# Splits and loads of an attention encoder in another order: key parts one per period, first casts of the drain, output weights ahead of the next chunk's rows

## The chip, the cores and the metric

The kernel runs on one core of one Trainium2 chip. The metric is the device time of one execution in microseconds. Engines are named as in the profile: PE (TensorE), DVE (VectorE), ACT (ScalarE), POOL (GpSimd) and SP (SyncE, which here only issues DMAs, in order).

## What is computed

A two-layer encoder runs over a prompt of 2048 tokens and a sample of 512 tokens, each of 1024 channels, in float32. Layer 0 is windowed attention with 16 heads, 4 key-value heads, blocks of 128 queries, a bias by relative position, a sink logit per head and a SiLU gate. Layer 1 mixes by a Fourier transform over positions and channel groups, gated as well. The core of layer 0, cut:

```python
h = rmsnorm(x, g)
z = h @ w_in                       # q, k, v and gate, one product
scores = einsum("bnqhgd,bnkhd->bnhgqk", q, k) * scale + bias   # |i-j| <= 128
p = exp(scores - m); p = p / (sum(p) + exp(sink - m))
o = einsum("bnhgqk,bnkhd->bnqhgd", p, v)
return x + (o * silu(gate)) @ w_out
```

## The kernel before

Every float32 product is made of three products of halves: an operand is split into a high half, which ACT makes by a cast to fp32r, and a low half, which DVE or POOL makes by subtracting the high half from the operand. `matmul3` (L137) multiplies the halves; `beside` (L522) takes two products at a time, one on the upper and one on the lower 64 rows of the array, and lets their matmuls alternate.

Layer 0 works through five chunks of 512 tokens: chunk 0 is the sample, chunks 1 to 4 are the prompt. A chunk begins with `make_h` (the rows xk of x transposed are loaded by SP at L275, multiplied by the inverse norm on POOL at L277, split by ACT at L281 and DVE at L282) and `kv_proj` (keys into kwin, values into v). Then a loop `for n in range(19)` runs: 16 periods and three of drain. Each period executes a list of names, `PERIOD` for chunks 1 to 4 and `FIRST` for chunk 0; beside each name stands how many periods back its unit lies. Calls of `seq` chain the instructions of each engine in the order of this list, so that the list is the order of the work. One unit is half of a head pair's work. The names:

- S1 and S2 are the score products (PE, L655, into the banks spt). b1a to b2b add the bias and find the maximum (DVE, L674, CUSTOM), e1a to e2b are the exponentials (ACT, L682), r1 and r2 the reciprocals (DVE, L688), m1a to m2b the divides (DVE, L697 and L701; ACT, L695).
- T0 and T1 transpose the probabilities into the one buffer tp (PE, L714); hi0, hi1 (ACT, L727) and lo0, lo1 (DVE, L731) split tp into pts. T1 can write tp only when lo0 has read it.
- AV1 and AV2 multiply by the values (PE, L755); they need lo1 and lo0. t2, add, mul, sp and lop take the result on to uT (ACT L775, DVE L785, POOL L791, ACT L796, POOL L800).
- A and B are the projections of later heads (PE, L522): q and gate go into two banks, pj0 and pj1, alternately. qH and qL evacuate them: in chunks 1 to 4 by `evac_q` (ACT L565 reads the bank for the high half, DVE L566 reads it again for the low half) or `evac_g`; for the head pair p = 1 by `evac_first`, where ACT copies the bank (L579), ACT casts the copy (L580) and DVE subtracts (L581). In chunk 0 the list's "sc" reads the bank first, DVE L585 for q and L596 for the gate s, and qH and qL follow on the copy (L590, L601).
- W and WL split weights (ACT L180, POOL L185); "side" does odd jobs in chunk 0, late weights (POOL L937) and the key parts.

Key parts: in chunk 0 the keys lie in two buffers kt; eight parts of them have to be split into kwin, high half by ACT (L401) and low half by DVE (L402), both in `part_k`. Two are done before the loop, six at "side" in the first four periods, two, two, one and one.

Between two chunks stands the output projection of the chunk before (`out_proj`): eight steps of products of uT with wo, whose second half of the weights (wo_1_0 to wo_1_6) is loaded by `rest`, its first step, into four buffers. SP issues loads in order, and each waits for its buffer. In chunks 2 to 4 `make_h` comes ahead of `rest` and the other steps.

Of the kernel before, what the change touches and what calls it, by code (L numbers as in the profile page):

```python
# [20 lines left out]
P = 128  # L21
# [34 lines left out]
def encoder(  # L56
# [150 lines left out]
    def attention_phase():  # L207

        with ExitStack() as es:
# [5 lines left out]
            def stats(c):  # L215

                tok, lo_t, hi_t = CHUNKS[c]
                nt = min(640, hi_t - tok) // P
                ss = main.tile([P, 8], F32, tag="ss", bufs=2, name=f"ss{c}")

                xs = []

                def one(i):

                    if i:
                        sq = ACT.activation(xs[i - 1], xs[i - 1], AF.Square, accum_out=ss[:, i - 1 : i])

                        if c > 1:
                            seq(ACT, sq)
                        else:  # L230
                            after(sq, last_exp[0])
                    while len(xs) < min(nt, i + (2 if c > 1 else 1)):
                        t = len(xs)
                        xs.append(xtile([P, D], F32, f"xs{c}_{t}"))
                        after(SP.dma_start(xs[t], x[tok + t * P : tok + (t + 1) * P, :]), last_exp[0] or last_x[0])

                return [lambda i=i: one(i) for i in range(nt + 1)] + [
                    lambda: inv_rms(ss, nt, f"inv{c}", lambda ins: seq(DVE, ins) if c > 1 else None)
                ]

            def spread_all(c, inv):
# [146 lines left out]
            def kv_proj(c, hs, halo, norms=None, early=None):  # L388
# [9 lines left out]
                def part_k(t, j, rows, src):  # L398
                    kw, sp = kwin[2 * t + j], src[j * 64 : j * 64 + 64, :n]
                    cs = slice(own0 + P, own0 + P + n)  # L400
                    hi = ACT.copy(kw[rows, 0, cs], sp)  # L401
                    lo = DVE.tensor_tensor(kw[rows, 1, cs], sp, f32(kw[rows, 0, cs]), ALU.subtract)  # L402
                    if PE in chain:
                        seq(ACT, hi)
                        seq(DVE, lo)

                def evac_k(t, ps, n, wc):
                    ps = scaled(ps, invb, f"k{t}")
# [66 lines left out]
                if norms is not None:  # L475
                    for t in range(2):
                        kt = main.tile([P, 512], F32, tag="xr", bufs=3, name=f"kt{c}_{t}")
                        DVE.tensor_tensor(kt, kps[t], invb[:, :CH], ALU.mult)
                        for j in range(2):
                            for rows in (slice(0, 64), slice(64, 128)):  # L480
                                k_splits.append(lambda t=t, j=j, rows=rows, kt=kt: part_k(t, j, rows, kt))
                    for _ in range(2):
                        k_splits.pop(0)()
                if halo:
                    pt = spt[0][:, :256]
                    for t in range(2):
# [49 lines left out]
            def qg_proj(c, which, p, bank, hs, res, invb=None):  # L536

                n = 12 + p if which == "g" else p
                st = {}

                def fetch():
                    if "w32" not in st:
                        st["w32"] = fetch_w(n, f"{which}{c}_{p}")

                def high():
                    st["w"], low = split_w(c, n, f"{which}{c}_{p}", st["w32"])
                    return low

                def load():
                    st["w"] = load_w(c, n, f"{which}{c}_{p}", None if p else DVE, w32=st.get("w32"))  # L550

                def left(k):
                    ks = slice(k * P, (k + 1) * P)
                    return [t[:, ks] for t in st["w"]]

                out = Product(bank, left, lambda k: hs[k])

                def pair_of():
                    qab = ap.tile([P, 2, CH], F32R, align_bytes=LINE, tag="qab", bufs=2, name=f"qab{c}_{p}")
                    res["q"] = qab  # L560
                    return qab

                def evac_q():
                    st["qab"] = qab = pair_of()
                    seq(ACT, ACT.activation(qab[:, 0], out.ps, AF.Copy, scale=-0.125))  # L565
                    return lambda: seq(DVE, DVE.scalar_tensor_tensor(  # L566
                        qab[:, 1], out.ps, -0.125, f32(qab[:, 0]), ALU.mult, ALU.subtract
                    ))

                def evac_g():  # L570
                    th = ap.tile([P, CH], F32, tag="tmp", bufs=2, name=f"th{c}_{p}")
                    seq(ACT, ACT.activation(th, out.ps, AF.Tanh, scale=0.5))
                    s = res["s"] = ap.tile([P, CH], F32, tag="s", bufs=2, name=f"s{c}_{p}")
                    return lambda: seq(DVE, DVE.scalar_tensor_tensor(s, th, 1.0, out.ps, ALU.add, ALU.mult))

                def evac_first():
                    whole = ap.tile([P, CH], F32, tag="tmp", bufs=2, name=f"q{c}_{p}")
                    qab = pair_of()
                    seq(ACT, ACT.activation(whole, out.ps, AF.Copy, scale=-0.125))  # L579
                    seq(ACT, ACT.copy(qab[:, 0], whole))  # L580
                    return lambda: seq(DVE, DVE.tensor_tensor(qab[:, 1], whole, f32(qab[:, 0]), ALU.subtract))  # L581

                def normed_q():
                    whole = ap.tile([P, CH], F32, tag="tmp", bufs=2, name=f"q{c}_{p}")
                    place(DVE.scalar_tensor_tensor(whole, out.ps, -0.125, invb[:, :CH], ALU.mult, ALU.mult))  # L585

                    def high():
                        qab = pair_of()
                        seq(ACT, ACT.copy(qab[:, 0], whole))
                        return lambda: seq(DVE, DVE.tensor_tensor(qab[:, 1], whole, f32(qab[:, 0]), ALU.subtract))  # L590

                    return high

                def normed_g():
                    s = res["s"] = ap.tile([P, CH], F32, tag="s", bufs=2, name=f"s{c}_{p}")
                    place(DVE.tensor_tensor(s, out.ps, invb[:, :CH], ALU.mult))  # L596

                    def high():
                        th = ap.tile([P, CH], F32, tag="tmp", bufs=2, name=f"th{c}_{p}")
                        seq(ACT, ACT.activation(th, s, AF.Tanh, scale=0.5))  # L600
                        return lambda: seq(DVE, DVE.scalar_tensor_tensor(s, th, 1.0, s, ALU.add, ALU.mult))  # L601

                    return high

                def place(ins):
                    if PE in chain:
                        seq(DVE, ins)

                if invb is None:
                    evac = evac_g if which == "g" else evac_first if p == 1 else evac_q  # L610
                else:
                    evac = normed_g if which == "g" else normed_q
                return fetch, high, load, out, evac
# [453 lines left out]
            for c in range(len(CHUNKS)):  # L1067

                if c > 1:
                    hs, halo = make_h(c, invb)  # L1070
                for s in tail:
                    s()
# [73 lines left out]
                def side(n):  # L1146
                    if n in (1, 3):
                        side_steps.append(late_w(n // 2))
                    elif n in (2, 4):
                        side_steps.pop()()  # L1150
                    for _ in range((2, 2, 1, 1)[n] if n < 4 else 0):
                        k_splits.pop(0)()

                side_steps = []
                low_q, high_q, low_w = [], [], []
                for n in range(19):
                    if c == 0:
# [6 lines left out]
                    chain.setdefault(PE, None)  # L1164
                    first, second = fills(n)
                    if n == 16:
                        beside(*first[:2])
                        first = first[2:]
                    for name, back in PERIOD if c else FIRST:
                        m = n - back  # L1170
                        if name == "A":
                            beside(*first)
# [13 lines left out]
                        elif name == "WL":  # L1186
                            if low_w:
                                low_w.pop()()
                        elif name == "side":
                            side(n)  # L1190
                        elif name == "qL":
                            if low_q:
                                low_q.pop()()
                        elif name[:5] == "extra":
                            if n < 17:
                                for i in range(4 * n + 2 * int(name[5]), 4 * n + 2 * int(name[5]) + 2):
                                    extra(i)
                        elif 0 <= m < 16 and (name, m) != ("AV2", 15):
                            at[m // 2].ops[2 * (m % 2)][name]()
# [1073 lines left out]
```

## Time and profile before

| | |
|---|---|
| median of 3 runs | 1572.89 us (1572.43 to 1573.58) |
| the profiled execution | 1573.11 us |
| its span | 1571.3 us |
| granted TensorE clock | 0.999 |
| busy: PE, DVE, ACT, POOL | 98%, 73%, 57%, 29% of the span |

The rows of the profile read as follows. A timeline row gives the start in us, the duration in us, the engine, the line of the kernel, the operation, the tiles (out<-in) with their shape and a count, and in brackets how long the engine sat idle ahead of it and what ended that. A row of the waits gives the engine and line that waited, what it waited for, the total in us, how often, and the longest. A row of the groups gives the total busy time in us and the mean of one instruction in ns, then the idle time ahead.

### The profile page before, as it was taken

How to read it: one execution, taken by the hardware profiler on the slowest of the kernel's cores; microseconds unless marked ns; L12 is line 12 of the kernel's file. 1: busy time of each engine (PE TensorE's matmuls, PEld its weight loads, DVE VectorE, ACT ScalarE, POOL GpSimd, SP SyncE). 2: the span in 40 equal slices, each digit the busy share in tenths (PEclk: the TensorE clock that was granted, in tenths of full speed). 3: DMA queues.
4: the chain of work that ended last, by engine and by line, in shares of the span. 5: the costliest groups of instructions: out<-in, count | busy, mean ns of one | idle time of the engine just before them, and what ended most of it. 6: DMA issues, size and time to landing. Idle time of an engine off the chain costs nothing.

```text
span 1571.3 us, 33415 instructions
## 1 busy us (share of the span) xinstructions
PE 1545.5 (98%) x12958; PEld 1352.9 (86%) x12958; DVE 1147.0 (73%) x2503; ACT 892.3 (57%) x1960; POOL 454.1 (29%) x616
## 2 busy tenths in 40 slices
PE   9899999999999999999999999999999999999998
PEld 7799888999898888988888899988888888888886
DVE  5788655777637777367764477758999888989886
ACT  6788634777327785257861477746566564333353
POOL 2566562421413313314214142223121211101100
PEclk9999999999999999999999999999999999999999
DMA  8577687774766765856738666665575669656852
GB/s 327 208 273 232 218 344 276 230 277 168 280 237 203 253 217 188 335 199 196 264 130 337 234 224 233 233 250 192 211 251 184 205 239 397 211 201 246 298 193 94
DMA packets 100730, 372.70 MB, mean 237 GB/s; under 512 B 11235, under 2 KB 22251, under 8 KB 83420
## 3 DMA queue, kind: packets, MB, share of 16 engines
q1 hardware_dynamic: 82716, 297.38, 54.6%
q0 software_dynamic: 16688, 70.04, 11.3%
q10 hardware_dynamic: 1168, 3.15, 0.6%
q8 instruction: 102, 1.67, 0.4%
q14 instruction: 56, 0.46, 0.1%
HBM read 280.06 MB, written 90.47 MB: 236 GB/s over the span
## 4 chain that ended last, share of the span: by engine, by line
PE 83%; DVE 6%; DMA 5%; ACT 2%; issue 2%; POOL 1%; SPq 0%; POOLq 0%; DVEq 0%; ACTq 0%
PE pj L522 25%; PE av L755 6%; PE W L137 6%; PE pj L137 5%; PE spt L655 5%; PE tp L137 5%; PE av L137 5%; PE tp L714 4%; PE Wo L137 3%; PE spt L137 3%; PE Z L137 3%; PE fo L137 2%; PE z L1386 2%; PE Zo L137 2%; PE X L137 1%
## 5 line engine op out<-in xcount | busy, mean ns | idle before, releaser
L522 PE MATMUL pj<-h,wg 64*128 64x512 f32 x1920 | 438.7, 389 | 1.9 <-DVE s L596 1.9
L522 PE MATMUL pj<-h,wq 64*128 64x512 f32 x1560 | 379.7, 389 | 3.2 <-DVE q L585 3.2
L522 PEld LDWEIGHTS pj<-h,wg 64*128 64x128 f32 x1920 | 330.9, 184 | 26.7 <-DVE s L596 2.6
L522 PEld LDWEIGHTS pj<-h,wq 64*128 64x128 f32 x1560 | 284.4, 184 | 21.9 <-DVE q L585 3.9
L674 DVE CUSTOM_DVE_ANT_0 S<-spt,b 128x385 f32<-128x385 f32 (+1 forms) x320 | 165.3, 525 | 94.3 <-PE spt L655 90.8
L682 ACT ACTIVATE S<-S 128x385 f32<-128x385 f32 (+1 forms) x320 | 189.3, 592 | 64.8 <-DVE S L674 42.7
L727 ACT CAST pts<-tp 128x768 fp32r<-128x768 f32 (+1 forms) x160 | 121.2, 757 | 94.9 <-PE av L755 59.6
L731 DVE TENSOR_TENSOR pts<-tp,pts 128x768 fp32r<-128x768 f32 (+1 forms) x160 | 144.0, 900 | 13.2 <-ACT pts L727 12.4
L755 PE MATMUL av<-pts,v 64*128 64x256 f32 x1680 | 141.8, 287 | 0.4 <-DVE pts L731 0.4
L755 PEld LDWEIGHTS av<-pts,v 64*128 64x128 f32 x1680 | 126.3, 186 | 4.1 <-DVE pts L731 0.6
L800 POOL TENSOR_TENSOR uT<-o,uT 128x256 fp32r<-128x256 f32 x75 | 55.7, 743 | 247.0 <-ACT uT L796 246.7
L655 PE MATMUL spt<-kwin,qab 64*128 64x384 f32 (+1 forms) x960 | 121.1, 338 | 0.0
L137 PE MATMUL fo<-wo,tTu 128*128 128x512 f32 x480 | 115.1, 392 | 0.0
L714 PEld LDWEIGHTS tp<-ident,S 64*128 64x128 f32 x1792 | 91.9, 137 | 20.1 <-DVE pts L731 13.8
L714 PE MATMUL tp<-ident,S 64*128 64x64 f32 x1792 | 96.8, 224 | 7.9 <-DVE pts L731 7.4
L137 PEld LDWEIGHTS fo<-wo,tTu 128*128 128x128 f32 x480 | 88.3, 188 | 17.3
L791 POOL TENSOR_TENSOR o<-o,s 128x256 f32<-128x256 f32 x75 | 55.6, 742 | 121.1 <-DVE o L785 91.0
L697 DVE TENSOR_SCALAR S<-S 128x384 f32<-128x384 f32 (+1 forms) x192 | 89.0, 492 | 0.1
L655 PEld LDWEIGHTS spt<-kwin,qab 64*128 64x128 f32 x960 | 84.8, 187 | 2.3 <-issue 1.8
L522 PE MATMUL pj<-wo,uT 64*128 64x512 f32 x360 | 74.5, 390 | 0.0
L282 DVE SCALAR_TENSOR_TENSOR h<-xk,g0s,h 128x512 fp32r<-128x512 f32 x40 | 47.7, 1200 | 29.8 <-ACT h L281 29.7
L785 DVE TENSOR_TENSOR o<-av,t 64x256 f32<-64x256 f32 x150 | 62.0, 413 | 1.6 <-ACT t L775 0.5
(383 smaller groups left out, 3380.7 us busy)
## 6 DMA issues: line engine op xcount, KB each, us to landing
wo<-wsd SPq DMA_DIRECT2D x32, 1024.0 KB, 6.5
wq<-wsd SPq DMA_DIRECT2D x31, 1024.0 KB, 6.2
wg<-wsd SPq DMA_DIRECT2D x31, 1024.0 KB, 5.6
x<-x1d SPq DMA_DIRECT2D x40, 512.0 KB, 3.9
b<-b21d SPq DMA_DIRECT2D x40, 512.0 KB, 6.4
b<-rowd SPq DMA_DIRECT2D x40, 384.0 KB, 4.2
xs<-in_x_dram SPq DMA_DIRECT2D x23, 512.0 KB, 6.7
s2d<-gt POOLq DMA_DIRECT2D x40, 256.0 KB, 4.6
```

The costliest lines, as they stand in the source:

```text
L137: ins = pe(PE.matmul(out, a[i], b[j], start=start and i + j == 0, stop=stop and i == 1, skip_group_check=more))
L522: out.last[h] = pe(PE.matmul(out.ps, a[i], b[j], **out.flags()))
L655: pe(PE.matmul(spt[j][:, 2 + k0 * P : 2 + k1 * P], res["q"][rows, qp, b * P : (b + 1) * P], kwin[g][rows, kp, b * P + k0 * P : b * P + k1 ...
L674: seq(DVE, DVE.tensor_tensor_reduce(out=s[:, e0:e1], in0=ps[:, 1 + e0 : 1 + e1], in1=st["bias"][:, j, 386 - e1 : 386 - e0][:, ::-1], scale ...
L682: last_exp[0] = seq(ACT, ACT.activation(s[:, e0:e1], s[:, e0:e1], AF.Exp, bias=s[:, 386:387], scale=-1.0, accum_out=s[:, 387:388]))
L697: seq(DVE, DVE.tensor_scalar(s[:, ks], s[:, ks], den, None, ALU.mult))
L714: pe(PE.transpose(ps[h][:, kb, j, :], s[rows, j, 1 + kb * P : 1 + (kb + 1) * P], ident[rows, rows]))
L727: seq(ACT, ACT.copy(hi, ps))
L731: seq(DVE, DVE.tensor_tensor(lo, ps, f32(hi), ALU.subtract))
L755: last[i][h] = pe(PE.matmul(av[:, i, :256], v[rows], pt[rows], start=not swap and n == 0, stop=swap and n == len(todo[h]) - 1, skip_group_ ...
L785: seq(DVE, DVE.tensor_tensor(o[64 * j : 64 * j + 64], ps[0:64, :, j], t2[:, :, j], ALU.add))
L800: low = eng.tensor_tensor(lo, o, f32(hi), ALU.subtract)
```

## The change

Six edits of order, none of what is computed:

- The key parts go one per period. `part_k` issues the high half at "side" and returns the low half, which is issued at the next qL, behind the low half of q or gate.
- `evac_first` goes; the head pair p = 1 uses `evac_q` as the others do.
- From period 15 on, hi0 stands right behind T0 and lo0 right behind the two divides m2a and m2b.
- In period 16 one pair of products instead of two goes ahead of the list, and the other into A.
- In chunks 2 to 4 the first step of the output part, `rest`, is emitted ahead of `make_h`.
- The inverse norm and the squares of chunk 1 join the chains of DVE and ACT, as those of chunks 2 to 4 do.

```diff
                         sq = ACT.activation(xs[i - 1], xs[i - 1], AF.Square, accum_out=ss[:, i - 1 : i])
-                        if c > 1:
+                        if c:
                             seq(ACT, sq)
...
-                    lambda: inv_rms(ss, nt, f"inv{c}", lambda ins: seq(DVE, ins) if c > 1 else None)
+                    lambda: inv_rms(ss, nt, f"inv{c}", lambda ins: seq(DVE, ins) if c else None)
...
                     hi = ACT.copy(kw[rows, 0, cs], sp)
-                    lo = DVE.tensor_tensor(kw[rows, 1, cs], sp, f32(kw[rows, 0, cs]), ALU.subtract)
                     if PE in chain:
                         seq(ACT, hi)
-                        seq(DVE, lo)
+
+                    def low():
+                        lo = DVE.tensor_tensor(kw[rows, 1, cs], sp, f32(kw[rows, 0, cs]), ALU.subtract)
+                        if PE in chain:
+                            seq(DVE, lo)
+
+                    return low
...
-                    evac = evac_g if which == "g" else evac_first if p == 1 else evac_q
+                    evac = evac_g if which == "g" else evac_q
...
                 if c > 1:
+                    tail.pop(0)()
                     hs, halo = make_h(c, invb)
...
-                    for _ in range((2, 2, 1, 1)[n] if n < 4 else 0):
-                        k_splits.pop(0)()
+                    if k_splits:
+                        k_lows.append(k_splits.pop(0)())
...
                     if n == 16:
-                        beside(*first[:2])
-                        first = first[2:]
-                    for name, back in PERIOD if c else FIRST:
+                        beside(*first[:1])
+                        first = first[1:]
+                    order = [a for a in (PERIOD if c else FIRST) if n < 15 or a[0] not in ("hi0", "lo0")]
+                    if n >= 15:
+                        for name, behind in (("hi0", ("T0",)), ("lo0", ("m2a", "m2b"))):
+                            at_ = max(i for i, a in enumerate(order) if a[0] in behind)
+                            order.insert(at_ + 1, (name, 1))
+                    for name, back in order:
...
                             if low_q:
                                 low_q.pop()()
+                            if k_lows:
+                                k_lows.pop()()
```

The order of DVE's instructions in the first periods of chunk 0 before; q_1 is the bank read (L585), qab_1 its low half, kwin<-kt a key part's low half, pts_0_0 the transposes' low half, ISA the bias:

```order
L701 TENSOR_SCALAR S_0_0_575<-S_0_0_575 128x256
L402 TENSOR_TENSOR kwin<-kt_0_453,kwin 64x512 x2
L585 SCALAR_TENSOR_TENSOR q_1_627<-pj_73,invb_391 128x512
L688 RECIPROCAL S_0_1_612<-S_0_1_612 128x2
L701 TENSOR_SCALAR S_0_1_612<-S_0_1_612 128x384 x2
L674 ISA S_0_3_677<-spt_75,b_0_479 128x257
L674 ISA S_0_3_677 128x1
L674 ISA S_0_3_677<-spt_74,b_0_479 128x257
L674 ISA S_0_3_677 128x1
L731 TENSOR_TENSOR pts_0_0_629<-tp,pts_0_0_629 128x2x4x64
L590 TENSOR_TENSOR qab_1_679<-q_1_627,qab_1_679 128x512
```

The same place in the changed kernel, whose line numbers are a few lower:

```order
L699 TENSOR_SCALAR S_0_0_575<-S_0_0_575 128x256
L583 SCALAR_TENSOR_TENSOR q_1_624<-pj_73,invb_391 128x512
L686 RECIPROCAL S_0_1_612<-S_0_1_612 128x2
L699 TENSOR_SCALAR S_0_1_612<-S_0_1_612 128x384 x2
L672 ISA S_0_3_674<-spt_75,b_0_479 128x257
L672 ISA S_0_3_674 128x1
L672 ISA S_0_3_674<-spt_74,b_0_479 128x257
L672 ISA S_0_3_674 128x1
L729 TENSOR_TENSOR pts_0_0_626<-tp,pts_0_0_626 128x2x4x64
L588 TENSOR_TENSOR qab_1_676<-q_1_624,qab_1_676 128x512
L406 TENSOR_TENSOR kwin<-kt_0_453,kwin 64x512
```

The two low halves ahead of the bank read are gone from there; one stands behind the low half of q, ahead of the next reciprocal, and one in each of the five periods that follow.

DVE in period 15 of chunk 2, before; pts_7_0 is lo0 and the ISA rows on S_7_2 are the bias of the scores of the last head pair:

```order
L697 TENSOR_SCALAR S_7_1_8616<-S_7_1_8616 128x384 x2
L674 ISA S_7_2_8692<-spt_75,b_7_8185 128x385
L674 ISA S_7_2_8692 128x1
L731 TENSOR_TENSOR pts_7_0_8645<-tp,pts_7_0_8645 128x2x6x64
L674 ISA S_7_2_8692<-spt_74,b_7_8185 128x385
```

And in the changed kernel:

```order
L695 TENSOR_SCALAR S_7_1_8612<-S_7_1_8612 128x384 x2
L729 TENSOR_TENSOR pts_7_0_8641<-tp,pts_7_0_8641 128x2x6x64
L672 ISA S_7_2_8689<-spt_75,b_7_8181 128x385
L672 ISA S_7_2_8689 128x1
L672 ISA S_7_2_8689<-spt_74,b_7_8181 128x385
```

The low half has passed the first bias of its period; in chunk 0 it passes both.

SP's queue at the change from chunk 3 to chunk 4, before; xk are the rows for `make_h`, wo_1 the second half of the output weights:

```order
L161 DMA wo_1_0_11917<-wsd_118 128x2048
L275 DMA xk_4_11875<-in_xT_dram 128x512
L275 DMA xk_5_11881<-in_xT_dram 128x512
L275 DMA xk_6_11887<-in_xT_dram 128x512
L275 DMA xk_7_11893<-in_xT_dram 128x512
L161 DMA wo_1_2_11919<-wsd_119 128x2048
L161 DMA wo_1_4_11927<-wsd_120 128x2048
L161 DMA wo_1_6_11953<-wsd_121 128x2048
```

And in the changed kernel:

```order
L161 DMA wo_1_0_11863<-wsd_118 128x2048
L161 DMA wo_1_2_11865<-wsd_119 128x2048
L161 DMA wo_1_4_11873<-wsd_120 128x2048
L161 DMA wo_1_6_11899<-wsd_121 128x2048
L275 DMA xk_4_11925<-in_xT_dram 128x512
L275 DMA xk_5_11931<-in_xT_dram 128x512
L275 DMA xk_6_11937<-in_xT_dram 128x512
L275 DMA xk_7_11943<-in_xT_dram 128x512
```

Three loads of weights have passed the last four rows; in chunks 2 and 3 it is two, wo_1_4 and wo_1_6. On POOL of chunk 4 three loads of xr have passed the multiplies of these four rows, and on DVE the splits of these four rows now stand behind the output part's first evacuations. On PE the only move is the pair of period 16, six matmuls that stood ahead of AV1 and now stand behind AV2.

More of the change, by code (lines that the diff above doesn't have):

```diff
@@ L482, in kv_proj @@
                     for _ in range(2):
-                        k_splits.pop(0)()
+                        k_splits.pop(0)()()
                 if halo:
@@ L574, in evac_g @@
                     return lambda: seq(DVE, DVE.scalar_tensor_tensor(s, th, 1.0, out.ps, ALU.add, ALU.mult))
[L576 to L581, printed above, removed]
                 def normed_q():
@@ L1150, in side @@
                         side_steps.pop()()
-                    for _ in range((2, 2, 1, 1)[n] if n < 4 else 0):
-                        k_splits.pop(0)()
-                side_steps = []
+                    if k_splits:
+                        k_lows.append(k_splits.pop(0)())
+                side_steps, k_lows = [], []
                 low_q, high_q, low_w = [], [], []
```

## The prediction

> **What bounds the kernel now.** The page comes first. TensorE is busy nearly all of the span:
>
> ```profile
> PE 1545.5 (98%) x12958; PEld 1352.9 (86%) x12958; DVE 1147.0 (73%) x2503; ACT 892.3 (57%) x1960; POOL 454.1 (29%) x616
> ```
>
> The span is 1571.3 us, so PE's idle time is 25.8 us in all, and no edit of the order of the work can bring more than that. The profiled execution took 1573.11 us, 0.22 above the median of the runs (1572.89); sums below are made against 1573.11. A measurement of this kernel can tell about 0.2% (3.1 us) from no change. The second view is the list of PE's waits by what released them:
>
> ```profile
> PE tp L714 <- DVE pts L731: 7.4, 9, 1.4
> PE pj L522 <- DVE q L585: 3.2, 3, 1.5
> PE pj L522 <- DVE s L596: 1.9, 2, 1.2
> PE tp L137 <- DMA wo<-wsd: 1.0, 2, 0.9
> ```
>
> The change aims at these four rows, 13.5 us. They fall in four places, and the timeline says in which: the early periods of chunk 0, the second period of chunks 1 to 4, the drain of every chunk, and the output part between chunks.
>
> **Part 1, key parts one per period (chunk 0).** The timeline of PE shows five waits for the DVE read that frees a projection bank:
>
> ```profile
> 47.11 0.50 PE L522 MATMUL pj<-h,wq 64*128 64x512 f32 x1 [1.36 <-DVE q L585]
> 57.40 0.50 PE L522 MATMUL pj<-h,wg 64*128 64x512 f32 x1 [1.20 <-DVE s L596]
> 67.56 0.50 PE L522 MATMUL pj<-h,wq 64*128 64x512 f32 x1 [1.51 <-DVE q L585]
> 77.35 0.50 PE L522 MATMUL pj<-h,wg 64*128 64x512 f32 x1 [0.74 <-DVE s L596]
> 138.27 0.49 PE L522 MATMUL pj<-h,wq 64*128 64x512 f32 x1 [0.33 <-DVE q L585]
> ```
>
> DVE's timeline shows why. The low halves of the key parts (L402) stand in its order ahead of that read and wait for ACT's high halves:
>
> ```profile
> 44.73 1.60 DVE L402 TENSOR_TENSOR kwin<-kt,kwin 64x512 fp32r<-64x512 f32 x2 [1.14 <-ACT kwin L401]
> 46.36 0.69 DVE L585 SCALAR_TENSOR_TENSOR q<-pj,invb 128x512 f32<-128x512 f32 x1
> ```
>
> The change puts each low half behind the low of q or g (L590, L601), a period after its cast, so the bank is read as soon as it is full. The first four waits are 4.8 us, and each is followed by a matmul of 0.50 us where its neighbours take 0.39, 0.4 more. The fifth is the inverse norm of chunk 1, which now stands behind the read: 0.3, with its slow matmul 0.4. Together 5.6. In the first period the read alone (0.69) may still end just behind PE's arrival; I leave 0.2 to it.
>
> What is added is one low half of 0.69 in each of periods 1 to 6, later in the chain of DVE that ends in the second transposes' low half, for which AV1 waits. How much room that has is seen in a later period without key parts:
>
> ```profile
> 106.14 0.17 DVE L688 RECIPROCAL S<-S 128x2 f32<-128x2 f32 x1 [0.22 <-ACT S L682]
> 107.30 0.56 DVE L674 CUSTOM_DVE_ANT_0 S<-spt,b 128x385 f32<-128x385 f32 x1 [0.24 <-PE spt L655]
> 108.26 0.95 DVE L731 TENSOR_TENSOR pts<-tp,pts 128x768 fp32r<-128x768 f32 x1
> 109.83 0.63 PE L755 MATMUL av<-pts,v 64*128 64x256 f32 x6
> ```
>
> DVE is idle for 0.46 on the way, and its low half ends at 109.21, 0.62 before AV1. That is 1.08 of room against 0.69: hidden. Two periods differ, since there POOL splits a late weight right behind the ordinary split. In the second of them before shows what that does:
>
> ```profile
> 66.77 2.82 POOL L937 TENSOR_TENSOR latelo<-w32late,latehi 128x256 fp32r<-128x256 f32 x4
> 69.98 0.68 DVE L590 TENSOR_TENSOR qab<-q,qab 128x512 fp32r<-128x512 f32 x1
> 86.74 2.82 POOL L937 TENSOR_TENSOR latelo<-w32late,latehi 128x256 fp32r<-128x256 f32 x4
> 87.52 2.59 DVE L590 TENSOR_TENSOR qab<-q,qab 128x512 fp32r<-128x512 f32 x1
> 92.93 0.62 PE L755 MATMUL av<-pts,v 64*128 64x256 f32 x5 [0.37 <-DVE pts L731]
> ```
>
> The DVE instruction that takes 0.68 alone took 2.59 beside POOL and ended 0.55 after POOL's four pieces. The Trainium skill has the rule for it ("SBUF — State Buffer", Who interferes with whom): a DVE instruction with both inputs in SBUF contends with a GpSimd instruction that reads SBUF, and whichever starts first keeps the other out. These rows agree, four POOL pieces holding out one DVE instruction. The rule speaks against this part, since a key low reads both its inputs from SBUF; taken at its worst it gives the first rival below.
>
> With the wait at 67.56 gone, the L590 of 69.98 comes 1.5 earlier, at 68.5, under the POOL run that ends at 69.59. It then ends 1.1 later than it would, and with the low's 0.69 behind it and 0.6 to 1.1 of room that is a new wait of 0.7 to 1.2 at AV1; I take 1.1. In the second period 0.37 is lost already, so the low comes on top: 0.7. Net of part 1: 5.6 − 0.2 − 1.8 = 3.6. Bounds: 5.4 if neither collision bites, 1.5 if each of the other four lows also loses 0.5.
>
> **Part 2, q of the second period (chunks 1 to 4).** PE waits at the second transposes:
>
> ```profile
> 268.38 0.59 PE L714 MATMUL tp<-ident,S 64*128 64x64 f32 x12 [1.12 <-DVE pts L731]
> 477.36 0.58 PE L714 MATMUL tp<-ident,S 64*128 64x64 f32 x12 [1.35 <-DVE pts L731]
> 689.67 0.59 PE L714 MATMUL tp<-ident,S 64*128 64x64 f32 x12 [1.35 <-DVE pts L731]
> 896.43 0.59 PE L714 MATMUL tp<-ident,S 64*128 64x64 f32 x12 [1.23 <-DVE pts L731]
> ```
>
> That is 5.05 us. ACT and DVE of chunk 2 lead up to it:
>
> ```profile
> 472.35 0.60 ACT L579 ACTIVATE q<-pj 128x512 f32<-128x512 f32 x1 [0.35 <-PE pj L522]
> 472.98 0.62 ACT L580 CAST qab<-q 128x512 fp32r<-128x512 f32 x1
> 473.63 0.69 DVE L581 TENSOR_TENSOR qab<-q,qab 128x512 fp32r<-128x512 f32 x1 [1.43 <-ACT qab L580]
> 474.24 1.73 DVE L697 TENSOR_SCALAR S<-S 128x384 f32<-128x384 f32 x2
> 476.36 0.95 DVE L731 TENSOR_TENSOR pts<-tp,pts 128x768 fp32r<-128x768 f32 x1
> 473.09 0.39 PE L522 MATMUL pj<-h,wg 64*128 64x512 f32 x1
> L566 DVE SCALAR_TENSOR_TENSOR qab<-pj,qab 128x512 fp32r<-128x512 f32 x28 | 19.4, 691 | 22.7 <-ACT qab L565 22.7
> ```
>
> From q's low half on DVE runs without a gap to the low half at 476.36 that the transposes wait for. The change leaves out one of ACT's two instructions, so DVE starts 0.66 earlier at the same 0.69 (its group L566 has a mean of 691 ns), and the transposes come about 0.65 earlier. But the bank is now read by ACT and DVE, not by ACT alone: A, which started at 473.09 behind ACT, waits until DVE's read ends, 472.97 + 0.69 = 473.66, some 0.6 later. PE was ready for the transposes at 477.36 − 1.35 = 476.0; 0.6 later that is 476.6, just ahead of 477.36 − 0.65 = 476.7, when the low half lets them go. So PE exchanges 1.35 at the transposes for 0.6 at A and 0.1 there: the gain is 0.65, four times 2.6. It is 0 if POOL's split, which moves with ACT's cast, holds DVE for as much longer; at most 5.05 if all goes; and −2.4 if A's 0.6 is added and nothing comes off.
>
> **Part 3, the drain.** In period 15 the first low half of head 7 goes ahead of the bias (L674), and only one pair of products instead of two is left ahead of AV1 in period 16. The waits at the second transposes go; one of them, in chunk 2, with what DVE and PE do before it:
>
> ```profile
> 607.98 0.53 PE L714 MATMUL tp<-ident,S 64*128 64x64 f32 x10 [0.50 <-DVE pts L731]
> 602.55 0.95 DVE L731 TENSOR_TENSOR pts<-tp,pts 128x768 fp32r<-128x768 f32 x1
> 604.07 0.88 PE L755 MATMUL av<-pts,v 64*128 64x256 f32 x12
> ```
>
> All drains together hold 7.4 − 5.05 = 2.4 us. The pair moved behind AV2 is three steps of about 0.23 and fills the wait at 607.98; AV1 comes these 0.69 earlier, at 603.4 less what is won before it, and meets its low half, which ended at 603.50. I take a new wait of 0.3 to 0.6 in each drain, 1.9 in all: net +0.5, between −1.5 and +2.4.
>
> **Part 4, output part ahead of the rows (chunks 2 to 4).** On SP's queue the halves of wo come ahead of the rows xk:
>
> ```profile
> 832.00 4.73 SPq L275 DMA_DIRECT2D xk<-in_xT_dram  x4
> 842.97 0.50 PE L137 MATMUL tp<-wo,uT 128*128 128x512 f32 x1 [0.85 <-DMA wo<-wsd]
> 859.42 0.87 PE L137 MATMUL pj<-h,wk 128*128 128x384 f32 x4
> ```
>
> The waits of 1.0 go, and some slowed matmuls beside them: I take 1.9, bounds 1.0 and 1.9. Price: in chunk 4 the rows are issued only when the last half has its slot, some 5 us later (the halves went out behind the rows, from 832.00 + 4.73 on), and POOL's multiplies now stand behind loads of xr that wait for stores. Before, such loads ran until 856.66:
>
> ```profile
> 856.66 0.55 POOL L882 DMA_DIRECT2D xr<-in_x_dram  x1 [5.74 <-DMA x1d<-xr]
> 838.74 1.74 POOL L277 TENSOR_TENSOR xk<-xk,invb 128x512 f32<-128x512 f32 x1
> ```
>
> The evacuations ahead of them move up too, so I put POOL's release at 848; even at 856.66 the four multiplies, at 1.74 or less, end between 858.4 and 863.6. The products that read h begin at 859.4 with rows 0 to 3, which are ready. I count it as hidden, with up to 2 us if POOL comes free as late as that.
>
> **The sum.** 3.6 + 2.6 + 0.5 + 1.9 = 8.6, so 1573.1 − 8.6 = 1564.5.
>
> **The rivals.**
> - **POOL holds out every key low** (slower). If in all six periods the pair of lows on DVE loses the 1.9 that the L590 at 87.52 lost (2.59 − 0.69), each costs 0.69 + 1.9 − 0.62 = 2.0 at AV1, 12 in all. Part 1 is then 5.4 − 12 = −6.6, and with parts 2 to 4 (5.0) the time is 1574.7; with a gain of nothing in part 2 it is 1577.3. Slower begins at (5.4 + 5.0) / 6 = 1.7 a period. For it: the two L590 rows above. Against: the ordinary split runs end well ahead of the lows, and the L590 at 69.98 kept clear even of the late run, by 0.4. 6%.
> - **The wait of part 2 only moves.** POOL's split starts earlier with ACT's cast and DVE's divides end as late as before; A's 0.6 is then paid on top or inside the 1.35. Part 2 gives 0 to −2.4: 1567.1 to 1569.5. For it: the divides took 1.73 for two where they are beside POOL. 17%.
> - **The drain only moves,** AV1 waiting 0.7 in each: −1.1 rather than +0.5, 1566.1. 15%.
> - **The key lows cost more** in periods 1 to 6 than two collisions: part 1 at 1.5, 1566.6; with the last two together 1568 to 1571. 10%.
> - **More goes than I count:** no collision, all waits of the drain gone: 1573.1 − (5.4 + 2.6 + 2.4 + 1.9) = 1560.8. 10%.
>
> The order of instructions leaves no doubt that the moves are made. My forecast keeps 42%. The range takes in the neighbours on both sides, 1561.0 to 1569.3. Faster by over 0.2% means under 1569.7: all but the first rival and the tails of two others, 0.87; within 0.2% 0.09; slower 0.04, from the first.
>
> **What would show it.** Right: the waits at 47 to 78 us gone and no kwin low ahead of q; waits at AV1 in two early periods of about 1; in the second period of chunks 1 to 4 a wait of 0.6 at L522 and almost none at the transposes; wo waits gone and no PE wait for h in chunks 2 to 4. Wrong: waits at AV1 in all of periods 2 to 7, transposes in chunk 1 to 4 waiting as long as before, or kv products waiting for h.

## The result and the profile after

| | before | changed |
|---|---|---|
| median of 6 runs each | 1573.0 us (1571.51 to 1576.49) | 1564.56 us (1564.1 to 1566.59) |
| ratio, 95% interval | | 0.9947 (0.9934 to 0.996) |
| span of the profiled execution | 1571.3 us | 1562.3 us |

The changed kernel is 8.4 us faster by the medians and 9.0 by the two spans. The forecast was 1564.5. The page's first part, and PE's waits by what released them (total us, times, longest), now read:

```profile
PE 1545.1 (99%) x12958; PEld 1355.5 (87%) x12958; DVE 1148.0 (73%) x2503; ACT 889.3 (57%) x1956; POOL 454.5 (29%) x616
```

```profile
PE av L753 <- DVE pts L729: 3.0, 3, 1.4
PE pj L527 <- DVE qab L571: 1.2, 4, 0.4
PE spt L653 <- DVE S L672: 0.7, 2, 0.4
```

PE does the same work in the same busy time; what went is idle time. The four rows of 13.5 us that the prediction started from (transposes 7.4, q 3.2, s 1.9, wo 1.0) are gone from the list. Three new rows stand in their place, 4.9 us: AV1 waits for DVE, A waits for the second read of the bank, score products wait for the bias. A fourth, 0.3 for keys at the start of chunk 1, comes and goes between kernels that do not differ up to there.

PE has the same 12958 matmuls in both kernels, in the same order but for the pair of period 16. So the start of the i-th can be compared in both traces, and the gain read place by place. Each kernel has one trace, but the places repeat: in the kernels below, a place of the table that an edit leaves alone gains the same to 0.06 us. The exceptions are the kernel's first stage (from −1.6 to +0.4), the keys at the start of chunk 1 (−0.4 to +0.3), layer 1 (−1.1 to +1.2), and stretches of a lower clock in three of the traces, told of where they come. Gains in us, from matmul to matmul; a drain runs from the end of period 14 to the first products of the output part:

| place | gain | predicted |
|---|---|---|
| chunk 0, periods 0 to 14 | 3.7 | 3.6 |
| second period of chunks 1, 2, 3, 4 | 0.69, 0.66, 0.67, 0.68 = 2.70 | 2.6 |
| drains of chunks 0 to 4 | 0.15, 0.47, 0.23, 0.27, −0.17 = 0.95 | 0.5 |
| output part, chunk 1 to 2, 2 to 3, 3 to 4 | 0.33, 0.45, 1.15 = 1.9 | 1.9 |
| all else (first stage +0.1, keys of chunk 1 −0.3, layer 1 −0.2, other +0.1) | −0.3 | 0 |

An idle time costs more than its length. Matmuls of a projection start 0.23 us apart and last 0.39 in the profile, so the idle time begins 0.16 after the next one was due, and the first one after it takes 0.50 and holds up the one behind it by 0.1. The 0.85 at 842.97 in the kernel before, gone now, gave 1.15; even an idle time of 0.04 between chunks 1 and 2, whose cause the profile does not name, gave 0.33. The product behind it in the kernel before:

```profile
423.19 0.50 PE L137 MATMUL tp<-wo,uT 128*128 128x512 f32 x1
```

In chunk 0 the timeline of PE has no wait left at a projection; what it has instead is this:

```profile
70.81 0.39 PE L753 MATMUL av<-pts,v 64*128 64x256 f32 x2 [1.35 <-DVE pts L729]
89.64 0.62 PE L753 MATMUL av<-pts,v 64*128 64x256 f32 x5 [1.39 <-DVE pts L729]
174.36 0.39 PE L753 MATMUL av<-pts,v 64*128 64x256 f32 x2 [0.28 <-DVE pts L729]
```

The third lies in the drain; the first two are the two collisions that the prediction expected, and DVE and POOL show them. First DVE, the low half of q (L588) and the key low (L406), then POOL:

```profile
64.48 2.35 DVE L588 TENSOR_TENSOR qab<-q,qab 128x512 fp32r<-128x512 f32 x1
66.76 1.22 DVE L406 TENSOR_TENSOR kwin<-kt,kwin 64x512 fp32r<-64x512 f32 x1
...
83.37 2.19 DVE L588 TENSOR_TENSOR qab<-q,qab 128x512 fp32r<-128x512 f32 x1
85.57 1.13 DVE L406 TENSOR_TENSOR kwin<-kt,kwin 64x512 fp32r<-64x512 f32 x1
```

```profile
63.46 2.83 POOL L935 TENSOR_TENSOR latelo<-w32late,latehi 128x256 fp32r<-128x256 f32 x4
66.24 0.57 POOL L1141 DMA_DIRECT2D wsd<-latehi  x1
66.80 0.54 POOL L1141 DMA_DIRECT2D wsd<-latelo  x1
67.35 1.23 POOL L798 TENSOR_TENSOR uT<-o,uT 128x256 fp32r<-128x256 f32 x1
```

The low half of q ends 0.54 after POOL's split, as in the kernel before. The key low behind it is longer too, 1.22 instead of 0.69: it ends 0.64 after POOL's second DMA issue (67.34), and POOL's next instruction takes 1.23 where it takes 0.75 elsewhere. The last section says which of the two lengthened it.

In the second period of chunk 2 ACT has one instruction fewer, and DVE starts 0.63 behind ACT's start rather than 1.28:

```profile
467.20 0.60 ACT L570 ACTIVATE qab<-pj 128x512 fp32r<-128x512 f32 x1 [0.35 <-PE pj L527]
```

```profile
467.83 0.69 DVE L571 SCALAR_TENSOR_TENSOR qab<-pj,qab 128x512 fp32r<-128x512 f32 x1 [0.78 <-ACT qab L570]
468.44 1.71 DVE L695 TENSOR_SCALAR S<-S 128x384 f32<-128x384 f32 x2
470.55 0.95 DVE L729 TENSOR_TENSOR pts<-tp,pts 128x768 fp32r<-128x768 f32 x1
```

```profile
468.58 0.50 PE L527 MATMUL pj<-h,wq 64*128 64x512 f32 x1 [0.24 <-DVE qab L571]
471.55 0.59 PE L712 MATMUL tp<-ident,S 64*128 64x64 f32 x12
```

A waits for DVE's read at 468.58, and the transposes at 471.55 no longer wait. At the change from chunk 3 to chunk 4 SP and POOL show the rows behind the weights:

```profile
819.74 9.86 SPq L161 DMA_DIRECT2D wo<-wsd  x4
829.70 2.27 SPq L275 DMA_DIRECT2D xk<-in_xT_dram  x4
```

```profile
838.09 0.55 POOL L880 DMA_DIRECT2D xr<-in_x_dram  x1 [5.88 <-DMA x1d<-xr]
839.62 1.15 POOL L880 DMA_DIRECT2D xr<-in_x_dram  x2 [0.97 <-DMA x1d<-xr]
840.78 5.02 POOL L277 TENSOR_TENSOR xk<-xk,invb 128x512 f32<-128x512 f32 x4
```

```profile
842.88 5.47 DVE L282 SCALAR_TENSOR_TENSOR h<-xk,g0s,h 128x512 fp32r<-128x512 f32 x4 [11.30 <-ACT h L281]
```

```profile
850.85 0.87 PE L137 MATMUL pj<-h,wk 128*128 128x384 f32 x4
```

POOL comes free at 840.78, which is the forecast 848 less the 8.4 us that PE is ahead of the kernel before by then, within 1.2. The last row is split at 848.35, 2.5 us before the first product that reads any of them: the price of part 4 is hidden.

### The profile page after: what moved, and what is told of

It is laid out like the page before. It is cut to its first block, busy times and chain, and to the rows that moved or that the text cites. A ratio compares the mean times of both kernels' runs of the same rounds, so it can differ in the third digit from the quotient of the medians.

```text
span 1562.3 us, 33420 instructions
## 1 busy us (share of the span) xinstructions
PE 1545.1 (99%) x12958; PEld 1355.5 (87%) x12958; DVE 1148.0 (73%) x2503; ACT 889.3 (57%) x1956; POOL 454.5 (29%) x616
## 4 chain that ended last, share of the span: by engine, by line
PE 89%; DVE 6%; DMA 2%; ACT 1%; issue 1%; POOL 0%; POOLq 0%; ACTq 0%; DVEq 0%; SPq 0%
PE pj L527 27%; PE av L753 7%; PE W L137 6%; PE pj L137 6%; PE tp L137 5%; PE av L137 5%; PE spt L653 5%; PE spt L137 4%; PE tp L712 4%; PE Wo L137 3%; PE Z L137 3%; PE fo L137 3%; PE z L1392 2%; PE Zo L137 2%; PE X L137 1%; PE ABp L137 1%
## 5 line engine op out<-in xcount | busy, mean ns | idle before, releaser
L672 DVE CUSTOM_DVE_ANT_0 S<-spt,b 128x385 f32<-128x385 f32 (+1 forms) x320 | 165.1, 525 | 92.3 <-PE spt L653 88.3
L729 DVE TENSOR_TENSOR pts<-tp,pts 128x768 fp32r<-128x768 f32 (+1 forms) x160 | 144.1, 901 | 13.5 <-ACT pts L725 12.8
L281 ACT ACTIVATE h<-xk,g0s 128x512 fp32r<-128x512 f32 x40 | 28.8, 724 | 73.7 <-POOL xk L277 73.2
```

The source lines that it names most:

```text
L672: seq(DVE, DVE.tensor_tensor_reduce(out=s[:, e0:e1], in0=ps[:, 1 + e0 : 1 + e1], in1=st["bias"][:, j, 386 - e1 : 386 - e0][:, ::-1], scale ...
L729: seq(DVE, DVE.tensor_tensor(lo, ps, f32(hi), ALU.subtract))
```

## The experiments

The theory is that each part's gain stands by itself, in its own place, and that the two waits at AV1 come from POOL. The rivals: the gains lie elsewhere or only moved; and the key low is too long for its period by itself. Each kernel was timed in five rounds; medians of the kernel before were 1572.64 beside the first four, 1574.32 and 1574.09 beside the others, so ratios are compared.

**Each part undone.** Four kernels, each the changed one with one part as it was before.

```diff
-                    if k_splits:
-                        k_lows.append(k_splits.pop(0)())
+                    for _ in range((2, 2, 1, 1)[n] if n < 4 else 0):
+                        k_splits.pop(0)()()
```

> The changed kernel with the key parts put back (two, two, one and one in periods 0 to 3, high and low half together); the other edits stay. If the gain of chunk 0 is the bank reads freed from the key lows, less two collisions with POOL, the four waits of 0.7 to 1.5 us at the projections come back (5.6 with their slow matmuls), the two waits of 1.4 at AV1 shrink to one of about 0.4, and the time is 3.3 us longer than the changed kernel's: 1567.8. If the gain of chunk 0 came from elsewhere (squares and inverse norm of chunk 1), it stays within 1 us of 1564.5.

Measured: 1567.26 us, ratio 0.9966 (0.9953 to 0.9978). The waits are back and those at AV1 shrink:

```profile
PE pj L527 <- DVE q L583: 2.9, 2, 1.5
PE pj L527 <- DVE s L594: 1.9, 2, 1.2
...
PE av L753 <- DVE pts L729: 0.6, 2, 0.4
```

By the starts of matmuls periods 0 to 14 of chunk 0 gain 0.6 on the kernel before, where the changed kernel gains 3.7 (the first stage, which varies, left out of both). So the key parts make 3.2 of it. The remaining 0.6 lies around 138 us, where the inverse norm stood ahead of a bank read; that edit was not undone by itself.

```diff
-                    evac = evac_g if which == "g" else evac_q
+                    evac = evac_g if which == "g" else evac_first if p == 1 else evac_q
```

> The changed kernel with the evacuation of q of the second pair as before (ACT copies the bank, casts the copy, DVE subtracts). If one ACT instruction fewer ahead of DVE's low half is worth 0.68 in each of four chunks, the waits at the second transposes come back with 1.1 to 1.4 each, the waits for the bank in the same period go (0.24 to 0.41 idle), and the time is 2.7 longer: 1567.2. If the wait had only moved, the time stays at 1564.5.

Measured: 1566.74 us, ratio 0.9961 (0.9947 to 0.9975). The row of A's waits (1.2 in all) is gone and the transposes wait again; the wait in chunk 2 beside it:

```profile
PE tp L719 <- DVE pts L736: 5.0, 4, 1.4
```

```profile
472.51 0.58 PE L719 MATMUL tp<-ident,S 64*128 64x64 f32 x12 [1.34 <-DVE pts L736]
```

Each of the four periods is as long as before to 0.01 us, and the other places that the change touches are as in the changed kernel to 0.04. So 2.7 us belong to this edit, and PE exchanged 5.0 us at the transposes for 1.2 of idle time and slow first steps at A.

```diff
-                        beside(*first[:1])
-                        first = first[1:]
+                        beside(*first[:2])
+                        first = first[2:]
...
-                    if n >= 15:
+                    if n >= 19:
```

(The list keeps hi0 and lo0 in their places for all n.)

> The changed kernel with the drain as before (first casts in their old places, two pairs ahead of AV1). If the landmarks of the trace are right, the drain gave 1.1 over five chunks: the waits of 0.3 to 0.6 at the second transposes come back, the waits for the bias at the score products of chunks 2 and 3 (0.37 each) go: 1565.6. If the drain only moved its waits: 1564.5.

Measured: 1565.29 us, ratio 0.9951 (0.9936 to 0.9965). The drains are again as long as before, 1.0 in all, and the waits are as expected:

```profile
PE tp L712 <- DVE pts L729: 2.4, 5, 0.6
```

The medians alone (0.7 apart) would not show it; the starts of the matmuls do.

```diff
                 if c > 1:
-                    tail.pop(0)()
                     hs, halo = make_h(c, invb)
```

> The changed kernel with the first step of the output part emitted behind the rows again. If the loads of wo behind the rows on SP's queue cost what the landmarks say, waits for wo of about 0.05, 0.2 and 0.85 come back with slowed matmuls beside them and the time is 1.9 longer: 1566.4. If the later rows of the changed kernel cost something that hides part of the gain, the kv products start later there than this kernel's gain suggests and the difference is under 1 us.

Measured: 1566.33 us, ratio 0.9956 (0.9942 to 0.997).

```profile
PE tp L137 <- DMA wo<-wsd: 1.3, 2, 0.7
```

The output part is 1.0 longer than the changed kernel's between chunks 2 and 3 and 0.9 between 3 and 4, 1.9 in all. It is not the same 1.9 as the table's. Between chunks 1 and 2 the order is the old one again too, but PE has no idle time there, and the 0.33 stays. Between 2 and 3 PE waits 0.73 for wo, where the kernel before, with the same order of loads, waited 0.17; between 3 and 4 it is 0.59 against 0.85. So the waits that the old order makes vary from one kernel to the next by up to 0.6 (why is not shown), and against the kernel before the edit's own share is 1.6 to 1.9.

**What makes the waits at AV1.** The key lows left out of the two periods in which POOL splits the late weights:

```diff
-                            if k_lows:
-                                k_lows.pop()()
+                            if k_lows and n not in (3, 5):
+                                k_lows.pop(0)()
```

> The changed kernel, but the key lows leave out periods 3 and 5, in which POOL splits the late weights; they come in periods 1, 2, 4, 6, 7 and 8. If the two waits of 1.35 and 1.39 at AV1 are the key low on top of a held low half of q, each shrinks by the low's 1.1 to 1.2 us there, to about 0.2: chunk 0 is 2.3 shorter, 1562.2. If the held low half of q alone makes the waits, they stay and the time is 1564.5. If a low of 0.69 does not fit in any period, new waits appear at AV1 of periods 8 and 9.

Measured: 1561.36 us, ratio 0.9916 (0.9902 to 0.993), below the changed kernel's interval. The low half of q is held as long as ever, and the wait at AV1 is what that leaves:

```profile
64.97 2.35 DVE L588 TENSOR_TENSOR qab<-q,qab 128x512 fp32r<-128x512 f32 x1
```

```profile
70.15 0.62 PE L753 MATMUL av<-pts,v 64*128 64x256 f32 x5 [0.21 <-DVE pts L729]
```

Periods 0 to 14 of chunk 0 gain 6.1 on the kernel before (3.7 in the changed kernel): 2.4 from the two periods. No waits come in the later ones: a low of 0.69 fits where POOL does not hold it.

The other way round, POOL's split of the late weights placed behind the key low:

```diff
-                        pieces(lo, w32, f32(hi), ALU.subtract, 4)
...
+                        def pool():
+                            for j in range(4):
+                                cs = slice(j * 256, j * 256 + 256)
+                                after(POOL.tensor_tensor(lo[:, cs], w32[:, cs], f32(hi)[:, cs], ALU.subtract), chain[DVE])
```

(`pool` is called behind the key low at qL of periods 3 and 5, the stores a period later.)

> The changed kernel, but POOL starts its split of the late weights (periods 3 and 5) only behind DVE's key low of that period, and stores it a period later. If POOL's run is what holds the lows, the low half of q takes 0.69 instead of 2.2 to 2.35, the key low 0.69 instead of 1.1 to 1.2, both waits at AV1 go, and chunk 0 is 2.8 shorter: 1561.7. If POOL, pushed back by up to 2 us, then runs into the low half of the next period, part of it comes back as a wait a period later: 1563. If the lows themselves were too long for those periods, the waits stay.

Measured: 1566.99 us, ratio 0.9956 (0.9942 to 0.997), an interval that overlaps the changed kernel's. The median is 2.4 longer, but 1.4 of that is no doing of the edit: in this trace the granted clock fell to half for 3.4 us from 90.6 us on, and all six runs have a mean clock of 0.997 or 0.998 where the trace of the changed kernel has 0.999. The edit did not do what it was for: `after` only sets an order of issue, and between engines that makes nobody wait. POOL started 0.28 behind the low half of q and held it longer than before:

```profile
64.64 3.27 POOL L1143 TENSOR_TENSOR latelo<-w32late,latehi 128x256 fp32r<-128x256 f32 x4
```

```profile
64.36 2.96 DVE L588 TENSOR_TENSOR qab<-q,qab 128x512 fp32r<-128x512 f32 x1
67.25 1.21 DVE L406 TENSOR_TENSOR kwin<-kt,kwin 64x512 fp32r<-64x512 f32 x1
```

So the run tells nothing on the question it was made for, but shows the collision again, 2.96 instead of 2.35. The kernel that joins this edit to the casts from period 16 on, told of below, shares its fate:

> The last two together: if both effects stand by themselves, 2.8 and 0.7 add up and the time is 1561.0; it beats the changed kernel by 0.2%.

Measured: 1565.95 us, ratio 0.9944 (0.9931 to 0.9958). Its trace has two such stretches of half clock, at 71.8 and 92.3 us, and the same long lows (2.96 and 2.79). With a real wait in place of the order:

```diff
-                                after(POOL.tensor_tensor(lo[:, cs], w32[:, cs], f32(hi)[:, cs], ALU.subtract), chain[DVE])
+                                ins = POOL.tensor_tensor(lo[:, cs], w32[:, cs], f32(hi)[:, cs], ALU.subtract)
+                                tc.add_manual_dep(ins.ins, chain[DVE].ins.name, DONE, reason="behind the low")
```

> As the run that was to put POOL's split of the late weights behind the key low, but with a real wait of POOL for DVE's low (the run before it only placed it in POOL's order, and it started 0.3 behind the low half of q). If POOL's run is what holds the lows, both take 0.69 in periods 3 and 5, the waits of 1.4 at AV1 go, and chunk 0 is 2.5 to 2.8 shorter than the changed kernel's: 1562. If POOL, now later, holds the low half of the next period instead, waits at AV1 come one period later. If the lows are too long by themselves, the waits stay at 1.4: 1564.5.

Measured: 1563.05 us, ratio 0.9935 (0.9923 to 0.9947). Now POOL starts behind both lows, and both take 0.68 in period 3:

```profile
65.79 2.84 POOL L1144 TENSOR_TENSOR latelo<-w32late,latehi 128x256 fp32r<-128x256 f32 x4 [1.66 <-ACT S L680]
```

```profile
64.38 0.68 DVE L588 TENSOR_TENSOR qab<-q,qab 128x512 fp32r<-128x512 f32 x1
64.98 0.68 DVE L406 TENSOR_TENSOR kwin<-kt,kwin 64x512 fp32r<-64x512 f32 x1
...
73.86 1.64 DVE L406 TENSOR_TENSOR kwin<-kt,kwin 64x512 fp32r<-64x512 f32 x1
```

```profile
74.18 0.75 POOL L798 TENSOR_TENSOR uT<-o,uT 128x256 fp32r<-128x256 f32 x1
```

```profile
78.44 0.74 PE L753 MATMUL av<-pts,v 64*128 64x256 f32 x7 [0.53 <-DVE pts L729]
```

The two waits of 1.4 are gone: POOL's run made them, not the length of the lows. POOL, now later, holds the key low of the next period (1.64 at 73.86, beside the instruction at 74.18), which costs 0.53 there and 0.6 two periods on, where the same comes again. Periods 0 to 14 are 1.6 shorter than the changed kernel's, not 2.5 to 2.8: the outcome lies between the first and the second of the expectations.

**The two halves of the drain.** First the casts moved from period 16 on only, in chunks 1 to 4 (in chunk 0 from 15, as it was):

```diff
-                    if n >= 15:
+                    if n >= (16 if c else 15):
```

> The changed kernel, but in chunks 1 to 4 the first casts are moved from period 16 on, not from 15. If the low half ahead of the bias makes the waits of 0.37 at the score products of chunks 2 and 3, these go and the small waits of 0.15 at the transposes come back: 0.2 to 0.3 shorter in each of chunks 2 to 4, 0.7 in all, too little for the median (1563.9) and read from the starts of the same matmuls. If the waits come from the pair of period 16 they stay.

Measured: 1563.28 us, ratio 0.9928 (0.9916 to 0.9941). The row of waits for the bias (0.7 in all) is gone from the list. In the changed kernel the score products of period 15 in chunk 2 wait for a bank that the bias has to read, and the low half stands ahead of both biases' turns:

```profile
593.23 0.96 DVE L729 TENSOR_TENSOR pts<-tp,pts 128x768 fp32r<-128x768 f32 x1 [0.64 <-ACT pts L725]
594.10 0.55 DVE L672 CUSTOM_DVE_ANT_0 S<-spt,b 128x385 f32<-128x385 f32 x1
594.58 0.08 DVE L672 DVE_READ_ACCUMULATOR2_ANT S<- 128x1 f32 x1
594.58 0.56 DVE L672 CUSTOM_DVE_ANT_0 S<-spt,b 128x385 f32<-128x385 f32 x1
```

```profile
595.19 0.44 PE L653 MATMUL spt<-kwin,qab 64*128 64x384 f32 x2 [0.37 <-DVE S L672]
```

By the starts of the matmuls the drains of chunks 1 to 4 are 0.10, 0.30, 0.30 and 0.29 shorter than the changed kernel's, 1.0 in all. In those chunks this half of the edit was a loss. Then the pair:

```diff
-                        beside(*first[:1])
-                        first = first[1:]
+                        beside(*first[:2])
+                        first = first[2:]
```

> The changed kernel with two pairs of products ahead of the list in period 16 again; the first casts stay moved. If the pair is what fills the waits of 0.5 at the second transposes of the last period (0.6 in chunk 0), these come back, and the waits and slow starts at AV1 of the same period go: 0.3 to 0.5 longer in each of chunks 0 to 3, 1566. If the order of the casts does that alone, nothing changes: 1564.5.

Measured: 1565.57 us, ratio 0.9945 (0.9932 to 0.9958).

```profile
PE tp L712 <- DVE pts L729: 1.5, 3, 0.5
```

Three waits of 0.5 are back, in chunks 1 to 3, where the drain is 0.58, 0.54 and 0.57 longer; in chunk 4 it is 0.14 longer and in chunk 0 0.30 shorter. So beside the moved casts the pair gives 1.5, and the casts of period 15 in chunks 1 to 4 take 1.0 back.

**The best together.** Key lows left out of periods 3 and 5, casts from period 16 on in chunks 1 to 4:

> Key lows left out of periods 3 and 5, and first casts moved from period 16 on in chunks 1 to 4. If the effects of the two runs stand apart, they add up: 2.5 to 3 and 1.0 less than the changed kernel, 1560.6, the fastest so far; about 0.8% below the kernel before.

Measured: 1560.5 us (1559.51 to 1561.13), ratio 0.9917 (0.9904 to 0.9929). The interval lies below the changed kernel's 0.9934 to 0.996: this version beats both the kernel before and the changed one. By its ratio it cannot be told from the kernel that leaves out periods 3 and 5 alone (0.9916); by the starts of the matmuls both effects are there in full, each in its place. With POOL's wait in place of the left-out periods:

> POOL's wait for the key low, and first casts moved from period 16 on in chunks 1 to 4. If both hold: 1561, within 1 us of the kernel that leaves periods 3 and 5 out. If the wait of POOL only moves the collision: 1563.5.

Measured: 1562.21 us, ratio 0.9929 (0.9916 to 0.9942), behind the best as the collision of the next period says.

## Why the prediction was right

The total came out at 1564.56 for 1564.5, which is partly luck: the parts gave 9.3 where the sum had 8.6, places outside the parts took 0.3 back, and one trace is not the median.

- **Part 1** was forecast at 3.6 and gave 3.7, but by two errors that cancel. The freed bank reads and the inverse norm gave more than 5.4: at the projections PE gained 1.5, 1.7, 1.6 and 1.2, and 0.6 at the inverse norm, 6.6 in all. The forecast added 0.1 to each idle time, where about 0.3 went with it, and its 0.2 for the first period was not needed. Since more goes with an idle time than its length, PE's 25.8 us of idle time are not the bound that the prediction took them for. The two collisions with POOL took 2.9 instead of 1.8. Of that term the place, the cause and the order of size were right; its size was off because the key low was taken at its 0.69, where it took 1.22 and 1.13. The run with both periods left out gives these back, and the run with POOL behind the lows shows 0.68 for both. (Two small slips stand in its working: by its rows the L590 would end 1.0 later and not 1.1, and 3.6 less four times 0.5 is 1.6 and not 1.5.)
- **Part 2** was right in mechanism and size: A's wait takes part of what the transposes lose, 0.67 net per chunk against 0.65. The rival in which POOL's split moves with ACT's cast and holds DVE's divides as much longer did not come: the two divides take 1.71 (1.73 before) and start earlier.
- **Part 3** was forecast at +0.5 and gave 1.0, all of it undone with the edit. The waits at the transposes went, as said. New waits at AV1 of 0.3 to 0.6 in each drain were wrong: PE waited at AV1 in one drain, 0.28 in chunk 0. What came instead was not in the forecast: the score products of period 15 in chunks 2 and 3 wait for the bias that the moved low half delays.
- **Part 4** was right in mechanism: the waits for wo are gone, and the rows come 2.5 us ahead of their first reader. Its 1.9 in the table is three idle times of 1.06 in all and 0.3 that went with each, the upper of the two bounds; the 0.33 between chunks 1 and 2 is there without the edit too, so that the exact agreement is in part chance.
- **The rival on the slower side,** POOL holding every key low, had the mechanism right and the number of periods wrong: it held two of the six, as the forecast took it. In the four others the lows take 0.69. The Trainium skill's rule ("SBUF — State Buffer", Who interferes with whom) names what makes a low liable to it, two inputs in SBUF: the lows of chunk 0 take 0.68 to 2.96 in these runs, and q's low of chunks 1 to 4, which reads one input from PSUM, has the same duration all 32 times in the changed kernel, 8 of them beside a POOL instruction (its line's row, in ns, least, median and most):

```profile
L571 DVE SCALAR_TENSOR_TENSOR qab<-pj,qab x32: 691/692/693, 251.3 to 986.9; 128x512 fp32r<-128x512 f32 x32
```

The other half of the rule as the prediction gives it, that whichever starts first keeps the other out, is not what the starts in these traces show: lows that began 0.28 and 0.32 ahead of POOL were held all the same (2.96 and 1.64).

## What to carry to other kernels

Where an engine's order puts an instruction that waits for another engine ahead of the read that frees a bank, the wait of the bank is that engine's wait; issuing the second half of the split a period later removes it for the price of the instruction alone, as long as there is room in the chain where it lands. Look at what another engine runs at just that time: here two of six landing places cost 2.9 us of the 6.6 won, and leaving those two out gave the most of any later edit. To price a wait, count the idle time and the spacing that it breaks: here about 0.3 us more than the idle time. A set of moves should be undone one by one on the same matmuls' starts, since a half that loses 1.0 us can hide in a part that would gain 1.9 without it.

## What the runs showed of the hardware that was not expected

A DVE subtract with both inputs in SBUF, 0.68 alone, ended 0.54 to 0.56 after the last of four POOL instructions in a row, not after the first (2.35, 2.19 and 2.59 us); it took 2.96 when POOL began 0.28 behind it. A key low of the same kind that started 0.04 before a POOL DMA issue of 0.54 took 1.22 and ended 0.64 after it, with POOL's next instruction stretched from 0.75 to 1.23. The issue was not what held it, which leaves that instruction, though no run tried it apart: in the kernel before, the L590 at 69.98 took its 0.68 (the row stands in the prediction) beside two such issues.

```profile
69.54 0.57 POOL L1142 DMA_DIRECT2D wsd<-latehi  x1
70.11 0.54 POOL L1142 DMA_DIRECT2D wsd<-latelo  x1
```

In three of the traces the granted clock fell to half for 3.41 us in the middle of chunk 0: with the output part undone at 91.1 us, with POOL's split placed by order alone at 90.6, and in the kernel that joins that to the later casts at 71.8 and 92.3. PE's matmuls started 0.43 us apart there where 0.23 is usual, and each stretch cost 1.4 to 1.6 us. The runs of one kernel differ by as much: those of the changed kernel with a mean clock of 0.999 took 1564.1 to 1564.67, and the two with 0.998 took 1565.92 and 1566.59. What brings such a stretch on is not shown.
